# A recurrent hybrid layer on one core: the last product of each seven-product group moved into the next group, with two steps moved from GpSimd to VectorE

## The chip, the cores and the metric

The kernel runs on one core of a Trainium2 chip. A core has TensorE (matmuls into PSUM), VectorE (DVE in the profile), ScalarE (ACT), GpSimd (POOL) and SyncE (SP, which here only issues the DMAs). Each engine works through its own instructions in order and waits at semaphores for the others. The metric is the device time of one execution in microseconds; of the kernel before the median of three runs is 1235.01 us (1233.07 to 1236.85).

## The reference, cut to what matters

One layer of a decoder on 2048 prompt tokens and 8 sequences of 8 sample tokens (2112 in all), width 1024, everything in fp32:

```python
xn = rms_norm(x, norm_pre)
z = xn @ w_in                                    # 1024 -> 4096: v_pool | g_pool | u_lru | g_lru, 1024 each
d = mean over windows 2/4/8/16 of v_pool - v_pool       # one window for each group of 256 channels
y_pool = (d @ pool_w[group]) * pool_scale
xs = causal_conv4(u_lru)                         # depthwise, width 4
r, gi = sigmoid(xs @ wa + ba), sigmoid(xs @ wx + bx)    # block-diagonal, 8 heads of 128
a = exp(-8 * r * softplus(-lam)); u = xs * gi * sqrt(1 - a * a)
h_t = a_t * h_(t-1) + u_t                        # a scan over the tokens
mixed = concat(y_pool * silu(g_pool), h * silu(g_lru))  # 2048 wide
y = x + rms_norm(mixed @ w_out, norm_post)
```

The last rows of the pooling input, of the convolution input and of the scan are returned as well.

## The kernel before, in words

**Split products.** Every fp32 factor of a matmul is kept as a high part (fp32r, a cast) and a low part (the rest, one subtraction), and a product is three matmuls: high x high, high x low, low x high. A "split tile" for weights (`half_tile`, tag `w`) holds the two parts of a 512-deep by 128-wide piece.

**Blocks and quads.** The tokens lie along the free axis and are cut into three blocks of 704 (m = 0, 1, 2), each of two chunks of 352. The columns of `w_in` are cut into quads of 256: four each of V (pool input), G (pool gate), U (lru input) and L (lru gate). A quad of a block is an output of 2 x 128 columns by 2 x 352 tokens with 1024 as the contraction, seen as a 2 x 2 by 2 x 2 product of halves. Block 0 does it plainly, in eight products of 4 x 3 = 12 matmuls (`plain_slot`). Blocks 1 and 2 do it in seven products, the Strassen-Winograd way, from seven combinations of the weights and seven of x, the latter in the slots X11, T1, T2, X22, T3, X21, T4 of the tile XN (high and low part each). Product 1 goes into PSUM bank `a` and is copied to output quarter (0,0); product 6 is added to the same bank, which is copied to (0,1); then 7, which is added to (1,1); then 4, which is copied to (1,0). Products 5 and 3 share bank `e` in the same way, product 2 has bank `d`. So each addition to a bank must wait until the copy or sum of what the bank held is done (`evac` in `quad_slot`: `put_copy` on ACT, line 976; `put_sum` on DVE, line 972). The order of the seven is `ORDER = (1, 5, 6, 3, 7, 2, 4)`. After product 4 `quad_end` starts the quad's chain. Each block has 16 quads. Block 0's first three are done apart; the rest are counted from 0: quads 0 to 12 are of block 0, 13 to 28 of block 1, 29 to 44 of block 2; lasts[0] is quad 12, lasts[1] is quad 28.

**The chains.** Beside the products run generators that name an engine and a planned duration for each step: `pool_chain` (sums of windows on DVE, the high part `dh` on ACT, the low part `dl` on POOL, then four products with `pool_w` whose results are multiplied with the gate, line 1120), `conv_chain` (four taps, line 1145 on ACT and 1156 on DVE, high part `xh` on ACT, low part `xl` on POOL, then the gate products r and i), `lru_chain` (tanh tables; gi + 1 on ACT at line 1197, times xs on POOL at line 1199; exp, sqrt, the scan on DVE at line 1226, the gate on POOL), `silu_chain`, and `x_chain` (the next block's x: loads of tokens into the tiles A and B for the norm, their squares on ACT, then x itself into A and B, the norm's factors, eight scalings on DVE). `transition` then makes the seven split x tiles out of A, B and two "root" tiles.

**What sets the order.** A planner in Python writes all engines' instructions in order. For each slot (one product, `SLOT = 1.94` us planned, or a product and one chain product) `one_slot` emits the product, then the copies of the slot before, then prepares weights, and `run_jobs` grants steps of the chains by the time at which their engine and their input would be free. Counts of free tiles (`t_free`, `e_free`) hold a quad or a chain back: tag `t` has 17 tiles, `e` six, `w` six. A quad begins when two `t` tiles are free (for V: two `e` tiles and the pool chain before). Weights are asked for `AHEAD = 6` products ahead: `w_step` issues the DMA from scratch memory (`wsd`, line 870), or, where a combination is made for the first time, spawns its sums, its split and its store (line 827). All DMAs go through SP's queue in that order, and a DMA whose buffer isn't free holds up those behind it.

After the last quad the output projection (from line 1704 on) multiplies `mixed` with `w_out`, also by seven products, in an order that the framework's scheduler sets. Its accumulators lie in `t` and `e` tiles, its split inputs in `w` tiles.

## Time and profile before

| | |
|---|---|
| median of the runs | 1235.01 us (1233.07 to 1236.85) |
| the profiled execution | 1239.46 us, its span 1237.6 us |
| TensorE busy | 1147.4 us, 93% |
| VectorE busy | 905.7 us, 73% |
| ScalarE busy | 680.5 us, 55% |
| GpSimd busy | 347.1 us, 28% |
| DMA | 322.10 MB, 260 GB/s in the mean |

The stages in the profile: up to about 79 us the first three quads of block 0 with the start of the kernel, up to 312 the rest of block 0, up to about 594 block 1, up to about 880 block 2, then the output projection. A row of the timeline has the start, the duration, engine, line, operation, output<-inputs, shape, count, and in brackets the idle time before it with what ended it. Tile names: a1V is bank `a` of a V quad in block 1, w2L a weight tile of an L quad in block 2, XN an x tile, e, u and g the outputs of V, U and G or L quads. A wait's row has the engine and what it wanted, the releaser, then total us, times and the longest. "issue" is a wait whose releaser the profile doesn't show. SPq is SP's queue of DMAs.

### The profile page before, as it was taken

To read this page: it belongs to the slowest core of one execution; us is meant where nothing else is said; L and a number is where in the kernel's file an instruction comes from. 1 tells how busy PE (TensorE), PEld (TensorE's weight loads), DVE (VectorE), ACT (ScalarE), POOL (GpSimd) and SP (SyncE) were. 2 spreads that over 40 slices of the span, in tenths; PEclk is the share of its full clock that TensorE was granted. 3 is DMA by queue.
4 is the path that set the end of the run, shared out by engine and by line. 5 is a ranking of instruction groups with operands and counts; after the bars stand their busy time and mean duration, and the time that the engine had idled before them with its cause. 6 is when DMAs were issued, how large, how long until landed. Compare 5 with 4: busy or idle time off the path is not lost. (4 is left out here: it accounts for less than half of the span.)

```text
span 1237.6 us, 17847 instructions
## 1 busy us (share of the span) xinstructions
PE 1147.4 (93%) x6274; PEld 1064.7 (86%) x6274; DVE 905.7 (73%) x1308; ACT 680.5 (55%) x1138; POOL 347.1 (28%) x332
## 2 busy tenths in 40 slices
PE   7999996999799899999889889999999999979987
PEld 6999996999799899998789879999878888767866
DVE  6878674784984857688867849686676677768677
ACT  5358664856756747474677556657854233234222
POOL 4223022221351221413542516354120012212232
PEclk9999997999999999998999999999999999989998
DMA  9277894676689788978689999997879676566553
GB/s 336 99 271 271 309 364 163 245 274 229 248 321 375 271 293 282 336 266 307 203 300 339 381 309 359 346 314 276 229 211 264 189 209 192 170 212 189 161 176 120
DMA packets 173305, 322.10 MB, mean 260 GB/s; under 512 B 17504, under 2 KB 79200, under 8 KB 173216
## 3 DMA queue, kind: packets, MB, share of 16 engines
q1 hardware_dynamic: 173216, 320.97, 76.4%
q8 instruction: 49, 0.80, 0.3%
q14 instruction: 40, 0.33, 0.1%
HBM read 218.51 MB, written 102.15 MB: 259 GB/s over the span
## 5 line engine op out<-in xcount | busy, mean ns | idle before, releaser
L437 POOL TENSOR_TENSOR xr<-ac,xr 128x512 f32<-128x512 f32 x27 | 49.5, 1854 | 239.4 <-issue 124.3
L444 PE MATMUL p<-XN,s 128*128 128x512 f32 (+1 forms) x224 | 88.2, 394 | 6.9 <-ACT s L131 6.6
L446 PE MATMUL p<-XN,s 128*128 128x512 f32 (+1 forms) x224 | 88.9, 397 | 5.2 <-DVE s L134 4.5
L1156 DVE SCALAR_TENSOR_TENSOR xs<-u,parT,xs 128x704 f32<-128x704 f32 (+1 forms) x72 | 91.3, 1280 | 1.9 <-ACT xs L1145 1.5
L445 PE MATMUL p<-XN,s 128*128 128x512 f32 (+1 forms) x224 | 87.8, 392 | 1.0 <-DVE XN L309 0.7
L1199 POOL TENSOR_TENSOR ig<-ig,xs 128x704 f32<-128x704 f32 (+1 forms) x24 | 44.8, 1869 | 143.6 <-ACT ig L1197 110.9
L557 ACT ACTIVATE p<-ac 128x512 f32<-128x512 f32 (+1 forms) x32 | 18.8, 588 | 99.2 <-DVE ac L437 98.7
L309 POOL TENSOR_TENSOR dl<-s,dh 128x704 fp32r<-128x704 f32 x24 | 40.6, 1693 | 105.5 <-ACT dh L1092 42.4
L1120 DVE SCALAR_TENSOR_TENSOR g<-y,parT,g 128x352 f32<-128x352 f32 x48 | 27.9, 581 | 56.9 <-PE y L240 56.9
L309 POOL TENSOR_TENSOR xl<-xs,xh 128x704 fp32r<-128x704 f32 (+1 forms) x24 | 48.7, 2030 | 70.1 <-ACT xh L1161 67.4
L240 PE MATMUL zL<-XN,wL 128*128 128x352 f32 x384 | 65.0, 329 | 0.0
L240 PEld LDWEIGHTS zL<-XN,wL 128*128 128x128 f32 x384 | 63.6, 193 | 0.0
L437 DVE TENSOR_TENSOR a<-a,a 128x512 f32<-128x512 f32 x48 | 35.4, 741 | 37.3 <-DMA a<-mixed 29.6
L444 PEld LDWEIGHTS p<-XN,s 128*128 128x128 f32 x224 | 43.3, 193 | 16.9 <-ACT s L131 7.7
L446 PEld LDWEIGHTS p<-XN,s 128*128 128x128 f32 x224 | 43.0, 192 | 16.9 <-DVE s L134 7.3
L131 ACT CAST s<-a 128x512 fp32r<-128x512 f32 x48 | 28.1, 615 | 53.6 <-DVE a L437 52.4
L240 PE MATMUL y<-dh,pw 128*128 128x352 f32 x192 | 54.0, 323 | 0.0
L446 PE MATMUL p<-XN,a 128*128 128x512 f32 x137 | 53.8, 393 | 0.0
L444 PE MATMUL p<-XN,a 128*128 128x512 f32 x137 | 53.6, 391 | 0.0
L445 PE MATMUL p<-XN,a 128*128 128x512 f32 x137 | 53.5, 391 | 0.0
L445 PEld LDWEIGHTS p<-XN,s 128*128 128x128 f32 x224 | 43.1, 192 | 11.3 <-DVE XN L309 1.2
L240 PE MATMUL zG<-XN,wG 128*128 128x352 f32 x288 | 48.8, 330 | 2.7 <-ACT wG L822 2.3
(347 smaller groups left out, 3433.4 us busy)
## 6 DMA issues: line engine op xcount, KB each, us to landing
a<-mixed SPq DMA_DIRECT2D x112, 256.0 KB, 4.2
mixed<-g SPq DMA_DIRECT2D x48, 352.0 KB, 5.6
w2V<-wsd SPq DMA_DIRECT2D x28, 512.0 KB, 4.9
w2G<-wsd SPq DMA_DIRECT2D x28, 512.0 KB, 5.9
w2U<-wsd SPq DMA_DIRECT2D x28, 512.0 KB, 5.8
w2L<-wsd SPq DMA_DIRECT2D x28, 512.0 KB, 6.3
wsd<-XN SPq DMA_DIRECT2D x27, 512.0 KB, 5.7
w1V<-wsd SPq DMA_DIRECT2D x24, 512.0 KB, 5.9
```

The source lines that it names most:

```text
L131: hi_eng.copy(out=hi, in_=src)
L240: nc.tensor.matmul(out, lhsT=lhsT, rhs=rhs, start=start, stop=stop)
L309: (eng or V).tensor_tensor(out=out, in0=a, in1=b, op=ALU.subtract)
L437: (eng or nc.vector).tensor_tensor(out=out, in0=a, in1=b, op=op)
L444: nc.tensor.matmul(out, lhsT=ah, rhs=wh, start=start and k == 0, stop=False)
L445: nc.tensor.matmul(out, lhsT=ah, rhs=wl, start=False, stop=False)
L446: nc.tensor.matmul(out, lhsT=al, rhs=wh, start=False, stop=stop and k == KT - 1)
L557: nc.scalar.activation(out=junk, in_=o, func=AF.Square, accum_out=st[:, g:g + 1])
L1120: V.scalar_tensor_tensor(out=g[:, cs], in0=Y, scalar=col(C_SCALE, blk), in1=g[:, cs], op0=ALU.mult, op1=ALU.mult)
L1156: V.scalar_tensor_tensor(out=xs, in0=E[:, k:k + n], scalar=col(C_CW + 8 * k, b), in1=xs, op0=ALU.mult, op1=ALU.add)
L1199: G.tensor_tensor(out=gi, in0=gi, in1=v, op=ALU.mult)
```

## The change

- **Order of products.** A quad of blocks 1 and 2 now does 1, 5, then product 4 of the quad before, then 6, 3, 2, 7. The first quad of block 1 has no quad before it, the last quad of all does its own 4 at the end. `steps` holds the new order, so weights are loaded by it too. If a quad cannot begin for want of tiles, the pending product 4 is emitted at once (`rest`), before the quad's own first product.
- **VectorE for GpSimd.** `dl`, the pool path's low part, is made by VectorE. The gated input becomes one VectorE instruction, (gi + 1) * xs, in place of one on ScalarE and one on GpSimd.
- **Table-aware order.** `run_jobs` adds 1.3 us to the start of a ScalarE step that needs another activation table, when it compares jobs.
- **x.** The load of a block's x is cut from two DMAs into four of two k-tiles each (eight over the two blocks), with 2.5 us planned after each. The x chain starts at quads 6 and 23 instead of 4 and 14. The turn to block 1 may begin one quad earlier, with X11, T1 and T2 not held back; the turn to block 2 has new slots for its parts, and it stretches over the last quad and the next.
- **Buffers.** `w` has seven tiles instead of six, `t` 16 instead of 17; the output projection's accumulators and one of its short inputs are placed anew to fit.

```diff
--- before.py
+++ after.py
@@ -57,7 +57,8 @@
 HOP = 0.2
 OVER = 0.7
 AHEAD = 6
-ORDER = (1, 5, 6, 3, 7, 2, 4)
+TABLE_COST = 1.3
+X_LEAD = (6, 5)
 XOF = {1: "X11", 6: "T2", 5: "T1", 7: "T3", 4: "T4", 2: "X21", 3: "X22"}
 SLOTS = ("A", "B", "X11", "T1", "T2", "X22", "T3", "X21", "T4")
 KINDS = {"V": 0, "G": 8, "U": 16, "L": 24}
@@ -389,14 +390,14 @@
     def acc_more():
         n = len(acc_all)
         n += 1
-        if n <= T_BUFS - 2:
+        if n <= T_BUFS - 1:
             t = t_tile(f"ac{n}")[:, :PIECE]
-        elif n == T_BUFS - 1:
+        elif n == T_BUFS:
             t = late[:, :PIECE]
-        elif n <= T_BUFS + E_BUFS - 4:
+        elif n <= T_BUFS + E_BUFS - 3:
             t = e_tile(f"ac{n}")[:, :PIECE]
         else:
-            n -= T_BUFS + E_BUFS - 3
+            n -= T_BUFS + E_BUFS - 2
             if n % 2 == 0:
                 acc_pair.append(half_tile(f"acw{n}"))
             t = acc_pair[n // 2][:, n % 2, :].bitcast(F32)
@@ -498,7 +499,7 @@
         n = hi - lo
         ts = []
         for e in range(2):
-            t = t_tile(f"as{q}_{e}", F32R)[:, :PIECE]
+            t = t_tile(f"as{q}_{e}", F32R)[:, :PIECE] if e else x2_box[0][:, 10 * PIECE:11 * PIECE]
             ts.append(t)
             r = stage(f"as{q}_{e}", e).rearrange("p (b t) -> p b t", t=P)[:, :, :n]
             b0 = 8 * q + 4 * e
@@ -782,10 +783,14 @@
             best = None
             for job in jobs:
                 s = fits(job, end)
-                if s is not None and (best is None or s < best[0] - 0.05):
-                    best = (s, job)
+                if s is None:
+                    continue
+                req = job["req"]
+                late = s + (TABLE_COST if len(req) > 2 and table[0] not in TABLES[req[2]] else 0.0)
+                if best is None or late < best[0] - 0.05:
+                    best = (late, s, job)
             if best:
-                grant(best[1], best[0])
+                grant(best[2], best[1])
                 moved = True
 
     def force(job):
@@ -862,9 +867,8 @@
 
     early = []
 
-    def w_step(q, i):
+    def w_step(q, pid):
         m, p, kind = q
-        pid = ORDER[i]
         t = w_tiles[q, pid] = half_tile(f"w{m}{kind}{p}_{pid}")
         if not is_late(q) or pid in (1, 2, 4):
             nc.sync.dma_start(out=flat_of(t).bitcast(F32), in_=w_key(kind, p, pid))
@@ -995,11 +999,8 @@
                 quad_end(q)
         return [("A", 0.45, evac)] if h else []
 
-    def quad_slot(q, i):
-        if q[0] == 0:
-            return plain_slot(q, i)
+    def quad_slot(q, pid):
         t = Q[q]
-        pid = ORDER[i]
         need_w(q, pid)
         w = w_tiles.pop((q, pid))
         key = {1: "a", 6: "a", 7: "a", 4: "a", 5: "e", 3: "e", 2: "d"}[pid]
@@ -1091,9 +1092,9 @@
             dh = e_tile(f"dh{m}_{p}{j}", F32R)[:, :MW]
             AC.copy(out=dh, in_=d)
             yield "?", lambda: e_free() >= 1
-            yield "G", 1.95
+            yield "V", 0.9
             dl = e_tile(f"dl{m}_{p}{j}", F32R)[:, :MW]
-            tsub(dl, d, dh.bitcast(F32), G)
+            tsub(dl, d, dh.bitcast(F32))
             e_live[0] -= 1
             Q[q]["d"].append((dh, dl))
         sums.add((m, p))
@@ -1193,10 +1194,8 @@
         n = MW if m < LM else N_LRU
         lq = (m, p, "L")
         b = 2 * p + j
-        yield "A", 0.89
-        AC.activation(out=gi, in_=gi, func=AF.Identity, bias=ones[:, 0:1])
-        yield "G", 1.95
-        G.tensor_tensor(out=gi, in0=gi, in1=v, op=ALU.mult)
+        yield "V", 0.95
+        V.scalar_tensor_tensor(out=gi, in0=gi, scalar=1.0, in1=v, op0=ALU.add, op1=ALU.mult)
         yield "A", 1.96, "exp"
         AC.activation(out=v, in_=r, func=AF.Exp, scale=nlam[:, b:b + 1], bias=nlam[:, b:b + 1])
         AC.activation(out=r, in_=r, func=AF.Tanh, scale=lam2[:, b:b + 1], bias=lam2[:, b:b + 1])
@@ -1262,9 +1261,12 @@
             for i in part:
                 yield "A", 1.06
                 tok_square(i)
-        yield "D", 0
         for h in range(2):
-            nc.sync.dma_start(out=stage_x(h), in_=xt[:, HK * h:HK * (h + 1), m * MW:(m + 1) * MW])
+            for k in range(0, HK, 2):
+                yield "D", 0
+                nc.sync.dma_start(out=stage_x(h)[:, k:k + 2, :],
+                                  in_=xt[:, HK * h + k:HK * h + k + 2, m * MW:(m + 1) * MW])
+                yield "t", 2.5
         yield "V", 0.2
         yield "A", 0.3, "sqrt"
         tok_rsqrt(tiles[0], tiles[-1] + 1)
@@ -1297,11 +1299,13 @@
         for o, a_, b_ in zip(parts(out), parts(a), parts(b)):
             tsub(o, a_, b_)
 
+    x_macro = [0]
+
     def transition(m):
 
         X = x_quarter
-        at = {0: {"X11": 0, "T1": 0, "T2": 0, "X22": 4, "T3": 5, "X21": 7, "T4": 9},
-              1: {"X11": 1, "T1": 2, "T2": 3, "X22": 4, "T3": 5, "X21": 6, "T4": 7}}[m]
+        at = {0: {"X11": -99, "T1": -99, "T2": -99, "X22": 4, "T3": 5, "X21": 7, "T4": 9},
+              1: {"X11": 1, "T1": 2, "T2": 4, "X22": 5, "X21": 6, "T3": 7, "T4": 10}}[m]
         src = {"X11": X(0, 0), "T1": X(0, 0), "T2": t2_tiles, "X22": X(1, 1), "T3": X(0, 1), "X21": X(1, 0),
                "T4": t2_tiles}
         done = set()
@@ -1333,11 +1337,12 @@
             x_raw(t2_tiles, X(1, 0), t2_tiles)
             x_jobs["X21"] = spawn(put("X21", "G"), T[0], rank=0)
             x_jobs["T4"] = spawn(put("T4"), clock["V"] + HOP, rank=0)
+        x_macro[0] = m + 1
         x_jobs["X11"] = spawn(put("X11"), rank=0)
         x_jobs["sums"] = spawn(chain(), rank=0)
 
     def need_x(n, m):
-        if "sums" not in x_jobs or slot_of[0] < 99:
+        if "sums" not in x_jobs or m != x_macro[0]:
             return
         if n != "X11":
             while n not in x_jobs:
@@ -1611,7 +1616,17 @@
             spawn(conv_chain((0, 0, "U"), j), 4.0)
 
         lasts = [i for i, q in enumerate(QUADS) if i + 1 == len(QUADS) or QUADS[i + 1][0] != q[0]]
-        steps = [(q, i) for q in QUADS if q[0] for i in range(7)]
+        slots, steps = [], []
+        for qi, q in enumerate(QUADS):
+            if q[0] == 0:
+                slots += [(qi, i, q, 0) for i in range(8)]
+                continue
+            seq = [(q, 1), (q, 5)] + ([(QUADS[qi - 1], 4)] if qi - 1 > lasts[0] else [])
+            seq += [(q, pid) for pid in (6, 3, 2, 7)]
+            if qi + 1 == len(QUADS):
+                seq.append((q, 4))
+            slots += [(qi, i, *s_) for i, s_ in enumerate(seq)]
+            steps += seq
         i0 = 8 * (lasts[0] + 1)
 
         def prep(n, qi, i):
@@ -1629,34 +1644,65 @@
             if n < len(steps):
                 w_step(*steps[n])
 
-        for n, (qi, i) in enumerate([(qi, i) for qi, q in enumerate(QUADS) for i in range(7 if q[0] else 8)]):
+        begun = [0, 0]
+
+        def x_turn(n, qi):
+
+            m = begun[0]
+            if m == 2:
+                return
+            if not begun[1]:
+                if m + 1 not in x_ready:
+                    if qi < lasts[m]:
+                        return
+                    while m + 1 not in x_ready:
+                        one_slot(None)
+                if qi < lasts[m] - (m == 0):
+                    return
+                transition(m)
+                begun[1] = 1
+            slot_of[0] = n - first_of[lasts[m]]
+            if slot_of[0] > 12:
+                begun[:] = [m + 1, 0]
+
+        first_of = {}
+        for n, (qi, i, _, _) in enumerate(slots):
+            first_of.setdefault(qi, n)
+        done = set()
+        for n, (qi, i, qp, pid) in enumerate(slots):
             q = QUADS[qi]
             m = q[0]
             if i == 0:
                 while t_free() < {"V": 0}.get(q[2], 2) or (q[2] == "V" and (e_free() < 2 or not sums_done(*q[:2]))):
-                    one_slot(None)
+                    rest = [s_ for s_ in slots[n:n + 3] if m and s_[2] != q and s_[2:] not in done]
+                    if rest:
+                        done.add(rest[0][2:])
+                        run_evacs(evacs)
+                        evacs.clear()
+                        one_slot(lambda: quad_slot(*rest[0][2:]))
+                    else:
+                        one_slot(None)
                 quad_begin(q)
                 while early:
                     force(early.pop())
                 if qi + 1 < len(QUADS) and QUADS[qi + 1][0] == 0:
                     w_raw(QUADS[qi + 1])
-            if i == (5 if m else 0) and qi + 2 < len(QUADS) and is_late(QUADS[qi + 2]):
+            if (pid == 7 if m else i == 0) and qi + 2 < len(QUADS) and is_late(QUADS[qi + 2]):
                 w_raw(QUADS[qi + 2])
-            if (m == 0 and (qi, i) == (4, 0)) or (m == 1 and (qi, i) == (lasts[0] + 2, 4)):
+            if m < LM and (qi, i) == (lasts[m] - X_LEAD[m], 0):
                 spawn(x_chain(m + 1), rank=0)
             if m == 2 and (qi, i) == (lasts[1] + 2, 0):
                 spawn(region_chain(0, "b11", 0, 5), then=[lambda: spawn(combos_chain())])
                 nc.sync.dma_start(out=stc, in_=st_conv)
                 nc.sync.dma_start(out=stl, in_=st_lru)
-            if qi in lasts[:2]:
-                slot_of[0] = i
-                if i == 0:
-                    while m + 1 not in x_ready:
-                        one_slot(None)
-                    transition(m)
-            else:
-                slot_of[0] = 99
-            one_slot(lambda: quad_slot(q, i), lambda: prep(n, qi, i))
+            x_turn(n, qi)
+            if (qp, pid) in done:
+                prep(n, qi, i)
+                continue
+            if pid == 4 and qp == q:
+                run_evacs(evacs)
+                evacs.clear()
+            one_slot(lambda: quad_slot(qp, pid) if m else plain_slot(q, i), lambda: prep(n, qi, i))
 
         def p1_slots(g):
             b = bank["a", g] = new_bank(f"p1_{g}")
@@ -1768,11 +1814,11 @@
             short_out()
 
 
-T_BUFS = 17
+T_BUFS = 16
 RAW_BUFS = 4
 TP_BUFS = 4
 E_BUFS = 6
-W_BUFS = 6
+W_BUFS = 7
 
 _OUTS = [
     ((T_ALL, D), "float32"),
```

## The prediction

> **What bounds the kernel now.** I read the page's busy times first, then the windows by stage, then TensorE's waits, then the timeline around the longest of them.
>
> ```profile
> span 1237.6 us, 17847 instructions
> PE 1147.4 (93%) x6274; PEld 1064.7 (86%) x6274; DVE 905.7 (73%) x1308; ACT 680.5 (55%) x1138; POOL 347.1 (28%) x332
> 79.00:312.00 233.00, 219.71 (x1338) 217.47 (x1337) 165.63 (x222) 152.54 (x253) 57.89 (x51) 0.96 0.72 262
> 312.00:594.00 282.00, 262.53 (x1550) 256.78 (x1549) 212.92 (x262) 171.75 (x265) 85.06 (x73) 0.96 0.86 302
> 594.00:880.00 286.00, 263.50 (x1567) 257.26 (x1566) 207.97 (x261) 183.69 (x276) 116.34 (x128) 0.98 0.89 313
> 880.00:1238.00 358.00, 332.62 (x1432) 267.60 (x1431) 262.38 (x452) 135.90 (x276) 66.14 (x40) 0.97 0.65 190
> ```
>
> TensorE is the bound. The change adds and removes no matmul, so all that can move is TensorE's idle time and the slow spells behind it. Columns of a window are its length, then busy us of PE, PEld, DVE, ACT, POOL, then granted clock, DMA share and GB/s. Block 0 (79 to 312) has 13.3 us of idle TensorE, blocks 1 and 2 (312 to 880), where the product order changes, 568 - 526.0 = 42.0 us, the out-projection (from 880) 25.4 us. Of TensorE's waits from 312 to 880 the short ones on x tiles and weights (total, times, longest), and from its timeline the longest waits of all kinds, each in brackets with its releaser:
>
> ```profile
> PE a2L L238 <- DMA w2L<-wsd: 1.0, 1, 1.0
> PE e2V L238 <- DVE XN L309: 0.9, 1, 0.9
> PE d2V L238 <- DMA w2V<-wsd: 0.9, 1, 0.9
> PE e2L L238 <- DMA w2L<-wsd: 0.8, 1, 0.8
> ```
>
> ```profile
> 317.79 3.38 PE L238 MATMUL e1V<-XN,w1V 128*128 128x352 f32 x11 [3.28 <-DVE XN L309]
> 328.40 2.03 PE L238 MATMUL d1V<-XN,w1V 128*128 128x352 f32 x11 [1.11 <-POOL XN L309]
> 339.38 3.89 PE L238 MATMUL a1G<-XN,w1G 128*128 128x352 f32 x12 [2.96 <-ACT g L976]
> 420.10 2.08 PE L238 MATMUL a1U<-XN,w1U 128*128 128x352 f32 x12
> 422.01 2.08 PE L238 MATMUL e1U<-XN,w1U 128*128 128x352 f32 x12
> 428.01 3.89 PE L238 MATMUL a1U<-XN,w1U 128*128 128x352 f32 x12 [3.91 <-ACT u L976]
> 564.58 3.89 PE L238 MATMUL a1U<-XN,w1U 128*128 128x352 f32 x12 [2.88 <-ACT u L976]
> 610.64 3.05 PE L238 MATMUL a2V<-XN,w2V 128*128 128x352 f32 x12 [3.71 <-issue]
> 700.05 3.66 PE L238 MATMUL a2L<-XN,w2L 128*128 128x352 f32 x12 [2.08 <-DVE g L972]
> 742.02 3.86 PE L238 MATMUL a2V<-XN,w2V 128*128 128x352 f32 x12 [4.82 <-DMA w2V<-wsd]
> 762.97 2.20 PE L238 MATMUL a2G<-XN,w2G 128*128 128x352 f32 x12 [2.40 <-DVE g L972]
> ```
>
> Two things are to be seen. One product is 12 matmuls of 2.08 us, and the next starts 1.92 us later (420.10, 422.01). And after a gap of some 2 to 5 us the next product mostly takes 3.05 to 3.89 us instead of 2.08: the clock is down (after 2.40 us once it was not).
>
> Of the 42.0 us, the split x tiles (XN) take 3.3 + 1.1 + 0.9 = 5.3, weights still in flight 4.8 + 1.0 + 0.9 + 0.8 = 7.5, the unnamed one 3.7. The remaining 25.5 us are accumulations that wait until ACT or DVE (lines 976, 972) has copied the bank out: products 1, 6, 7, 4 share one PSUM bank, 5 and 3 another, and each must be read out before the next adds to it.
>
> **The change part by part.**
>
> **The order.** Before, 1 5 6 3 7 2 4: one product (1.92 us) stands between two on the same bank. After, 1 5 4' 6 3 2 7, with 4' of the quad before: two stand between everywhere. So each of these waits shrinks by 1.92 us. Five are longer, 3.91 + 2.96 + 2.88 + 2.40 + 2.08 = 14.23, of which 14.23 - 5 x 1.92 = 4.6 stays; the others go. Gain 25.5 - 4.6 = 20.9. Their slow spells go too: 3 x (3.89 - 2.08) + (3.66 - 2.08) + (2.20 - 2.08) = 7.1. Together 28.0, 0.9 for each of the 32 quads of blocks 1 and 2.
>
> In sentences of its own: the Trainium skill, "TensorE: Matmul & The Clock Gate", section "Part 1: The HAM clock gate", has the clock fall after an idle window of about 3.4 us, and warns of gaps above 3. By that rule only the 3.91 gap among these five would have paid, and the 7.1 would be 1.8. The gaps of 2.08, 2.88 and 2.96 with 3.66 to 3.89 behind them say otherwise, so the rows decide.
>
> The wait at 610.64 is product 4 too (behind 7's sum on DVE). It had product 2 ahead of it and now has the next quad's 1 and 5, and DVE was late for that sum after one instruction of 3.93 us. I count it whole: 3.71 + (3.05 - 2.08) = 4.7.
>
> ```profile
> 601.51 3.93 DVE L1156 SCALAR_TENSOR_TENSOR xs<-u,parT,xs 128x704 f32<-128x704 f32 x1
> ```
>
> **The price of the order** is that a quad's end, and with it the chains behind it and the release of its two tiles, comes three products (5.8 us) later, while the t tiles go from 17 to 16. Tiles are short already:
>
> ```profile
> L949 POOL COPY u<-hu 128x3 f32<-128x3 f32 x16 | 10.9, 694 | 35.4 <-DVE rg L1226 33.8 <-DVE w L1209 1.6
> 427.51 0.45 ACT L976 COPY u<-a1U 128x352 f32<-128x352 f32 x1 [2.75 <-DVE rg L1226]
> 699.48 0.51 DVE L972 TENSOR_TENSOR g<-a2L,g 128x352 f32<-128x352 f32 x1
> ```
>
> The first write into a U quad's tiles (16 copies, the 8 U quads of blocks 1 and 2) waits for a scan to free them. In the changed code a quad that finds fewer than two free tiles pulls 4' ahead of its own 1, directly behind 7. Then 4' waits at least for the sum (0.51, and 0.57 from its start to the matmul at 700.05), and the quad has the old single cover. I take this for the 8 U quads: 8 x (0.9 not gained + 0.6) = 12.0 lost. Ends: none pulled (0), all 32 at 0.9 + 1.92 (90).
>
> **x pieces and the earlier turn.** Block 1's splits may start a quad earlier, so the waits at 317.79 and 328.40 go: 3.28 + 1.11 + (3.38 - 1.92 for 11 matmuls) = 5.9. Block 2's turn keeps its start; its 0.9 stays. The x chain itself starts later (quad 6 for 4, 23 for 14), so its squares, eight scalings and loads leave the stretches behind quads 4 and 14 and meet others. Each block's x comes in four loads of 0.72 MB instead of two of 1.44 (eight pieces over both blocks), spread over the queue:
>
> ```profile
> 167.72 0.93 SPq L1267 DMA_DIRECT2D XA<-in_xt  x2
> 176.15 7.26 SPq L338 DMA_DIRECT2D wr0U<-in_w_in  x4
> 185.67 0.33 SPq L903 DMA_DIRECT2D pwr<-in_pool_w  x1
> 192.50 0.62 ACT L911 CAST pw<-pwr 128x512 fp32r<-128x512 f32 x1 [12.86 <-DMA pwr<-in_pool_w]
> 193.86 0.66 PE L240 MATMUL r<-xh,lw 128*128 128x352 f32 x1 [8.20 <-ACT xh L1161]
> ```
>
> Here 2.88 MB of x sit ahead of four weight loads, whose issue takes 7.26 us, and of the small pool weights; ACT waits 12.86 us for these with xh queued behind them, and TensorE 8.20. At 302 GB/s the burst is 9.5 us, a piece 2.4. Ends 0 (same bytes through the same engines) and 8.2; I take the middle, 4.1.
>
> **Seven split tiles.** Loads are asked for six products ahead into six buffers, so each waits for the product that has just been issued:
>
> ```profile
> SPq L870 <- PE a2U L238: 23.2, 14, 2.8
> 730.69 6.83 SPq L940 DMA_DIRECT2D sp<-in_st_pool  x2
> 737.61 0.38 SPq L870 DMA_DIRECT2D w2V<-wsd  x1
> ```
>
> With the seventh a load leaves one product (1.92 us) sooner, and what stands behind it on SP with it. The waits of 1.0, 0.9 and 0.8 go; the 4.82 at 742.02, where the state load held the queue for 6.83 us, falls by 1.92. Gain 4.6, upper end 7.5. In the out-projection a seventh tile may help its splits or reshuffle them: 0, ends -5 and +5 out of 25.4 idle.
>
> **Low parts and gated input on DVE.**
>
> ```profile
> L309 POOL TENSOR_TENSOR dl<-s,dh x24: 1421/1613/2143, 80.6 to 840.4; 128x704 fp32r<-128x704 f32 x24
> L1199 POOL TENSOR_TENSOR ig<-ig,xs x24: 1699/1748/2364, 101.4 to 890.8; 128x704 f32<-128x704 f32 x16, 128x728 f32<-128x728 f32 x8
> L1197 ACT ACTIVATE ig<-ig,ones 128x704 f32<-128x704 f32 (+1 forms) x24 | 21.4, 893 | 0.3
> L1074 DVE SCALAR_TENSOR_TENSOR s<-s,e 128x704 f32<-128x704 f32 (+1 forms) x24 | 21.8, 910 | 0.3
> L1156 DVE SCALAR_TENSOR_TENSOR xs<-u,parT,xs x72: 937/962/3929, 78.2 to 860.3; 128x704 f32<-128x704 f32 x48, 128x728 f32<-128x728 f32 x24
> L1156 DVE SCALAR_TENSOR_TENSOR xs<-u,parT,xs 128x704 f32<-128x704 f32 (+1 forms) x72 | 91.3, 1280 | 1.9 <-ACT xs L1145 1.5
> L1212 ACT ACT_TABLE_LOAD x24 | 30.8, 1283 | 0.4
> ```
>
> DVE gains 48 instructions of 0.91 = 43.7 us; ACT loses 21.4; POOL loses 48 of about 1.7 (some 81 of its 259 us from 79 to 880, a third). L1156 costs 91.3 where 72 medians make 69.3: 22 us lost in the slow cases (up to 3.93). If a third of that goes with POOL's third, DVE's net is 36, 6% on the 587 it does from 79 to 880. It is not the bound at 73%; what reaches TensorE lies between 0 and 36, and I take 5, because a bank's sum stands in DVE's queue behind the new instructions.
>
> **Table-aware order** may save some table loads of 1.28 us (24 at one line) and may put a copy behind a chain that needs no load. ACT's lag is counted in the bank waits; I take 0, ends -5 and +5.
>
> **Sum:** 28.0 + 4.7 + 5.9 + 4.1 + 4.6 - 12.0 - 5 = 30.3. The profiled execution took 1239.46 (its span and 1.9 around it) and would take 1209.2. It lies 4.45 above the median 1235.01, so on the runs' scale I forecast 1204.7.
>
> **The rivals.**
>
> **All cover holds** (17%). Nothing is pulled back, the x burst and the weight waits go whole, DVE costs nothing: 28.0 + 4.7 + 5.9 + 8.2 + 7.5 = 54.3, 1181. For it: lru chains lose a POOL and an ACT step, so tiles come free sooner. Against it: the waits for the scan.
>
> **The lag is not cover's** (14%). At 428.01 the copy itself waits 2.75 us for a tile that a scan frees; if such causes stand behind most bank waits, the lag grows with the cover, the 28.0 is not had, and 4.7 + 5.9 + 4.1 + 4.6 - 5 = 14.3 is left: 1221. Against it: most of these waits are under 1.92 us.
>
> **Product 4 pulled back nearly everywhere: slower** (13%). One tile less and two tiles held 5.8 us longer; at the head of most quads fewer than two are free, 4' stands directly behind 7 and waits 1.92 more than with product 2 between. A pulled quad then costs 0.9 + 1.92 = 2.8 against a gain of 42.3 without any (30.3 + 12.0): it decides from 16 of 32 quads. At 23: 64.4 - 42.3 = 22.1 slower, 1257. For it: the 33.8 us of waits for the scan. Against it: in block 1 the two root tiles are held for a far shorter time, since the x chain starts nine quads later.
>
> **The new DVE work reaches TensorE whole** (4%): 36 in place of 5, 1235.0 - (35.3 - 36) = 1235.7. It would if the POOL work that stays (low parts of xs, the gate products) held each new DVE instruction as it held L1156 in its slow cases. Against it: L1156's median of 962 beside its least of 937, so most of its 72 are not held.
>
> Beside it, in sentences of its own: the Trainium skill, "SBUF — State Buffer", section "Who interferes with whom", has a DVE instruction with two SBUF inputs and a GpSimd one that reads SBUF block each other for the whole of the one that came first. All 48 new instructions are of that kind, so this speaks against the change; if each were held for some 1.7 us, DVE would gain 82 us more. L1156's slow cases agree with the rule, its median says how seldom it strikes.
>
> **How the numbers follow.** The forecast has 52%, its own range 1190 to 1220 (half its gain and one and a half of it). 0.3% (3.7 us) is about what a measurement of this kernel can tell from no change. Faster takes the forecast, all cover, and most of the lag case: 80%. Same: the 4% and slivers of its neighbours, 6%. Slower: the pulled case and a little, 14%. The range for 8 in 10 leaves out the far half of the slower case and the best part of the fast one: 1172 to 1240.
>
> **What would show it.** Right: idle TensorE from 312 to 880 near 20 us (42 now); waits of a1, a2 products on ACT and DVE copies below 1 us each; no wait on weights but one; the 3.28 at block 1's first quad gone; DVE some 30 us busier, POOL 80 us less. Wrong: product 4 directly behind 7 in many quads, with a wait at each; new waits of gate or pool products on DVE's low parts; TensorE waiting at block 2's turn for x tiles because its chain started too late; or DVE's slow instructions as many as before.

## The result and the profile after

The changed kernel takes 1193.76 us (median; 1192.5 to 1198.13) where the kernel before took 1234.55 us beside it: a ratio of 0.9674, 95% interval 0.9645 to 0.9703. It is faster by 40.8 us; the forecast was 1204.7 us. Its profiled execution took 1194.03 us. The page's first lines, as for the kernel before:

```profile
span 1192.3 us, 17811 instructions
PE 1132.6 (95%) x6274; PEld 1055.3 (89%) x6274; DVE 902.9 (76%) x1356; ACT 653.8 (55%) x1109; POOL 253.3 (21%) x284
```

For a comparison by stage both traces are cut at the same products: the first one with zV, with a1V, with a2V and with p as its output (block 0 behind its first three quads, block 1, block 2, the out-projection up to TensorE's last matmul). The windows of the kernel before, and then those of the changed kernel, columns as in the prediction:

```profile
79.93:312.27 232.34, 219.23 (x1335) 217.28 (x1335) 164.97 (x221) 151.63 (x250) 58.16 (x51) 0.96 0.72 261
312.27:592.68 280.41, 260.94 (x1541) 255.19 (x1540) 211.33 (x260) 171.60 (x263) 84.37 (x73) 0.96 0.86 302
592.68:874.33 281.65, 259.15 (x1550) 254.02 (x1549) 206.54 (x260) 178.88 (x267) 116.50 (x128) 0.98 0.89 312
874.33:1228.92 354.59, 338.29 (x1457) 272.16 (x1456) 260.17 (x442) 138.89 (x277) 66.39 (x40) 0.98 0.67 194
```

```profile
79.62:311.18 231.56, 220.23 (x1335) 217.77 (x1336) 185.32 (x250) 153.09 (x252) 35.56 (x42) 0.97 0.73 266
311.18:570.19 259.01, 251.65 (x1540) 248.63 (x1539) 196.58 (x266) 170.35 (x266) 45.49 (x54) 0.99 0.91 323
570.19:843.65 273.46, 255.94 (x1555) 252.87 (x1554) 204.23 (x271) 154.92 (x242) 90.81 (x109) 0.98 0.88 324
843.65:1182.47 338.82, 334.64 (x1450) 269.35 (x1450) 253.60 (x443) 135.90 (x271) 59.85 (x38) 0.99 0.69 203
```

Block 0 gives 0.8 us, block 1 21.4, block 2 8.2, and the out-projection 15.8, for which the prediction had taken nothing. These are differences of one execution each, and the one before lies 4.9 us above its median of 1234.55, so they add up to some 46 us where the medians differ by 40.8. In blocks 1 and 2 TensorE's idle time falls from 42.0 to 24.9 us. Its busy time falls too, from 520.1 to 507.6 us for nearly the same matmuls (3091 and 3095 in the windows): 12.5 us less of slow clock. The middle of block 1 has no gap left (windows of 50 us; TensorE is busy for all of each):

```profile
361.00:411.00 50.00, 50.00 (x314) 50.00 (x313) 42.24 (x58) 32.87 (x51) 10.94 (x12) 1.00 0.90 309
411.00:461.00 50.00, 50.00 (x313) 50.00 (x312) 33.76 (x42) 26.27 (x42) 10.40 (x14) 1.00 0.88 297
461.00:511.00 50.00, 50.00 (x314) 50.00 (x313) 32.06 (x41) 33.67 (x51) 8.63 (x12) 1.00 1.02 387
```

TensorE's longest waits in the changed kernel (what it wanted, releaser, total, times, longest; one row of 2.4 us on y is left out):

```profile
PE a2V L239 <- DMA w2V<-wsd: 6.7, 2, 5.8
PE z L241 <- ACT w L1443: 5.4, 1, 5.4
PE e2V L239 <- POOL XN L310: 5.0, 1, 5.0
PE r L241 <- ACT xh L1162: 4.4, 1, 4.4
PE p L445 <- ACT s L132: 3.9, 1, 3.9
PE a1U L239 <- DVE u L976: 2.2, 1, 2.2
```

The waits of a-, e- and d-products on copies and sums (copies are at line 980 here, sums at 976), 25.3 us in the trace before, come to 4.2 us when all rows of this view are added. Of the waits that stood out before, "issue" and the x tiles at block 1's start are gone. But at the turn to block 2 those on x tiles have grown from 0.9 to 6.2 us, and in blocks 1 and 2 those on weights from 7.5 to 8.9. The rest of what is left lies at the kernel's start (z), in block 0 (r) and in the out-projection (p).

### The profile page after: what moved, and what is told of

It is laid out like the page before. It is cut to its first block, busy times and chain, and to the rows that moved or that the text cites. A ratio compares the mean times of both kernels' runs of the same rounds, so it can differ in the third digit from the quotient of the medians.

```text
span 1192.3 us, 17811 instructions
## 1 busy us (share of the span) xinstructions
PE 1132.6 (95%) x6274; PEld 1055.3 (89%) x6274; DVE 902.9 (76%) x1356; ACT 653.8 (55%) x1109; POOL 253.3 (21%) x284
## 5 line engine op out<-in xcount | busy, mean ns | idle before, releaser
L438 POOL TENSOR_TENSOR xr<-ac,xr 128x512 f32<-128x512 f32 x27 | 46.6, 1745 | 225.8 <-DVE ac L578 120.1
L1157 DVE SCALAR_TENSOR_TENSOR xs<-u,parT,xs 128x704 f32<-128x704 f32 (+1 forms) x72 | 85.3, 1193 | 12.0 <-ACT xs L1146 11.6
L310 POOL TENSOR_TENSOR xl<-xs,xh 128x704 fp32r<-128x704 f32 (+1 forms) x24 | 45.9, 1910 | 144.1 <-ACT xh L1162 93.9
L438 DVE TENSOR_TENSOR a<-a,a 128x512 f32<-128x512 f32 x48 | 32.9, 690 | 28.5 <-DMA a<-mixed 24.7
L241 PE MATMUL zU<-XN,wU 128*128 128x352 f32 x288 | 50.3, 329 | 0.0
L241 PE MATMUL zV<-XN,wV 128*128 128x352 f32 x288 | 48.1, 323 | 0.3 <-ACT wV L827 0.2
L241 PEld LDWEIGHTS zU<-XN,wU 128*128 128x128 f32 x288 | 48.1, 194 | 0.0
```

The costliest lines, as they stand in the source:

```text
L241: nc.tensor.matmul(out, lhsT=lhsT, rhs=rhs, start=start, stop=stop)
L310: (eng or V).tensor_tensor(out=out, in0=a, in1=b, op=ALU.subtract)
L438: (eng or nc.vector).tensor_tensor(out=out, in0=a, in1=b, op=op)
L1157: V.scalar_tensor_tensor(out=xs, in0=E[:, k:k + n], scalar=col(C_CW + 8 * k, b), in1=xs, op0=ALU.mult, op1=ALU.add)
```

## The experiments

All times are medians; a ratio is to the kernel before on the same chip in the same stretch of runs, with its 95% interval. Differences between kernels go by the ratios, 1% being 12.3 us. The table has the stages of each profiled execution, cut as above; "w" is the number of split tiles.

| kernel | w | block 0 | block 1 | block 2 | out-projection | time | ratio |
|---|---|---|---|---|---|---|---|
| before | 6 | 232.3 | 280.4 | 281.7 | 354.6 | 1230.7 to 1234.6 | 1 |
| changed | 7 | 231.6 | 259.0 | 273.5 | 338.8 | 1193.8 | 0.9674 |
| old_order | 7 | 231.9 | 254.3 | 284.6 | 337.3 | 1195.4 | 0.9715 [0.9677, 0.9754] |
| six_split | 6 | 231.0 | 258.3 | 276.3 | 349.0 | 1206.4 | 0.9807 [0.9773, 0.9840] |
| on_pool | 7 | 232.7 | 260.1 | 287.0 | 332.1 | 1206.7 | 0.9807 [0.9773, 0.9841] |
| buffers_only | 7 | 239.8 | 295.6 | 271.2 | 332.4 | 1230.6 | 0.9981 [0.9958, 1.0003] |
| gi_only | 6 | 219.6 | 289.2 | 279.0 | 351.3 | 1226.6 | 0.9955 [0.9934, 0.9976] |
| bgi | 7 | 220.5 | 286.0 | 271.5 | 333.5 | 1202.8 | 0.9771 [0.9738, 0.9804] |
| bgitab | 7 | 237.3 | 279.8 | 282.6 | 337.1 | 1225.6 | 0.9944 [0.9924, 0.9964] |
| x_old | 7 | 223.1 | 293.6 | 282.8 | 334.1 | 1226.3 | 0.9949 [0.9931, 0.9968] |
| turn_late | 7 | 231.4 | 302.0 | 280.5 | 335.9 | 1239.6 | 1.0071 [1.0045, 1.0098] |
| lead_14 | 7 | 230.3 | 253.2 | 278.2 | 336.5 | 1191.8 | 0.9694 [0.9660, 0.9729] |
| hop_25 | 7 | 236.0 | 260.3 | 285.5 | 336.3 | 1211.6 | 0.9863 [0.9820, 0.9907] |
| sp_two | 7 | 232.1 | 255.5 | 262.4 | 337.3 | 1180.7 | 0.9596 [0.9554, 0.9638] |

### The order alone undone: old_order

```diff
-            seq = [(q, 1), (q, 5)] + ([(QUADS[qi - 1], 4)] if qi - 1 > lasts[0] else [])
-            seq += [(q, pid) for pid in (6, 3, 2, 7)]
...
+            seq = [(q, pid) for pid in (1, 5, 6, 3, 7, 2, 4)]
...
-            if pid == 4 and qp == q:
-                run_evacs(evacs)
-                evacs.clear()
```

> The changed kernel with the order of the seven products put back to 1 5 6 3 7 2 4; all else stays changed. Theory (the second product of cover is what took the bank waits away): of the 21.4 and 8.2 us that blocks 1 and 2 lost, most come back, TensorE's waits on the copies out of banks a and e rise from about 4 to 20 us or more, and the time is 1215 to 1225. Rival (ACT's lag fell because of the other parts: two steps off ACT and POOL, fewer table loads): bank waits stay below 10 us and the time is below 1203.

It lost 0.4% (5 us), and the intervals of the two ratios overlap; block 1 is 4.7 us shorter, block 2 11.1 longer. In its profile TensorE's waits on copies and sums are as short as with the new order, 4.8 us in all; the longest are these, while the turn to block 2 has grown:

```profile
PE a1V L239 <- ACT e L980: 2.4, 1, 2.4
PE e2G L239 <- ACT g L980: 1.6, 1, 1.6
PE e2V L239 <- POOL XN L310: 7.2, 1, 7.2
```

So with one product of cover, as before, the copies are in time: with the other parts in place the waits are gone without the new order. (Waits on weights are 15.7 us for 8.9.) What the new order would do by itself in the kernel before, no run shows.

### The seventh split tile undone: six_split

```diff
-W_BUFS = 7
+W_BUFS = 6
```

> The changed kernel with six split weight tiles instead of seven. Theory A (the out-projection's gain of 15 us comes from the seventh tile, which lets its next split start sooner): some 15 us back there and 4 to 8 in the blocks, 1210 to 1217. Theory B (the prediction: the tile is worth 4.6 us, in the blocks alone; the out-projection gained by a reshuffle): 1196 to 1201, with the out-projection as short as in the changed kernel.

It lost 1.3% (16 us), between what the two theories gave. By stage, in one execution each, the blocks together are 1.7 us longer (765.7 for 764.0), the out-projection 10.1. There TensorE waits for the splits of its inputs again, and its clock is a little lower, 0.98 for 0.99 (rows of its waits, then the window of the out-projection):

```profile
PE s L453 <- DVE as L135: 3.4, 1, 3.4
PE p L445 <- ACT s L132: 2.1, 1, 2.1
PE p L447 <- DVE s L135: 2.1, 1, 2.1
```

```profile
844.56:1193.51 348.95, 339.72 (x1450) 271.33 (x1450) 257.26 (x443) 136.36 (x271) 62.69 (x38) 0.98 0.67 197
```

The table's column for the out-projection says the same of all fourteen kernels: with six split tiles 349.0 to 354.6 us, with seven 332.1 to 338.8. No kernel lies between. No new order of jobs is behind it either: in this kernel's trace all 6274 matmuls stand in the changed kernel's order, and up to the out-projection the other engines' instructions too, one load in SP's queue aside.

### VectorE's new work given back: on_pool

```diff
-            yield "V", 0.9
+            yield "G", 1.95
...
-            tsub(dl, d, dh.bitcast(F32))
+            tsub(dl, d, dh.bitcast(F32), G)
...
-        yield "V", 0.95
-        V.scalar_tensor_tensor(out=gi, in0=gi, scalar=1.0, in1=v, op0=ALU.add, op1=ALU.mult)
+        yield "A", 0.89
+        AC.activation(out=gi, in_=gi, func=AF.Identity, bias=ones[:, 0:1])
+        yield "G", 1.95
+        G.tensor_tensor(out=gi, in0=gi, in1=v, op=ALU.mult)
```

(In this kernel y comes out other than the reference's; no run shows why. No instruction is left out, so its time is used, with this reserve.)

> The changed kernel with dl again on POOL and the gated input again as an ACT and a POOL instruction. Theory A (the prediction: the move costs up to 5 us, as DVE's queue gets longer): 1189 to 1194. Theory B (the move gains, because DVE is held less by POOL and the chains get shorter): 1199 to 1210, with L1156's kind of instruction back near 1280 ns in the mean and more bank waits.

It lost 1.3% (16 us); by the table block 2 is 13.6 us longer and the out-projection 6.8 shorter. So VectorE's new work did not cost anything that shows; the sign of my 5 us is wrong, or hidden below what a new order of jobs does (hop_25). VectorE's busy time shows something that the prediction had too small. Its 48 new instructions take 45.6 us in the changed kernel, but without them it is as busy, 901.7 us for 902.9 (the page of this kernel):

```profile
PE 1132.8 (94%) x6274; PEld 1054.8 (88%) x6274; DVE 901.7 (75%) x1308; ACT 675.0 (56%) x1132; POOL 330.1 (27%) x332
```

With 77 us more work on GpSimd, the 1308 instructions that VectorE has in both kernels take 44 us longer.

### The buffers alone: buffers_only

The kernel before with the changed kernel's buffers, the accumulators placed to fit, and nothing else:

```diff
-T_BUFS = 17
+T_BUFS = 16
...
-W_BUFS = 6
+W_BUFS = 7
```

> The kernel before with the buffers alone changed: 7 split tiles, 16 t tiles, accumulators placed to fit. Theory A (the seventh tile makes the out-projection shorter): out-projection 340 us instead of 355, time 1213 to 1222. Theory B (worth 4.6 us in the blocks at most, and one t tile less costs some of it): 1228 to 1236.

It gained 0.2%, with 1 inside its interval. But that zero has two halves: the out-projection is 22.2 us shorter, and the blocks, 806.6 us for 794.4, 12.2 longer (the rest of the span moved by 2.0). The losses are in block 1:

```profile
PE r L240 <- ACT xh L1161: 16.3, 3, 8.4
PE a1L L238 <- ACT g L976: 8.6, 2, 8.0
```

### Built up from the kernel before: gi_only, bgi, bgitab

The kernel before with the gated input alone on VectorE; the same with the buffers; the same with the table-aware order as well. The edits are those of the change's diff.

> The kernel before with the gated input alone done on VectorE; seventeen t tiles and six split tiles as before, no other part of the change. Theory T (tiles: the seventh split tile pays in the out-projection and is paid for in the blocks by the t tile given up; the work taken off ScalarE and GpSimd brings the t tiles back sooner and repays that): 1215 to 1226 us, blocks 0 to 2 together 6 to 15 us shorter, the out-projection still 350 to 357 us. Rival X (blocks 1 and 2 gain from the x chain and the turn to the next block, the move itself is worth little): 1228 to 1234 us.

> The kernel before with the gated input on VectorE and with sixteen t tiles, seven split tiles: the two parts that theory T says need each other. T: 1200 to 1212 us, so a gain larger than the 1.4 us of the tiles alone and that of the move alone taken together, the out-projection 330 to 340 us with no waits in it, blocks 0 to 2 together no longer than before. Rival X: 1220 to 1231 us, with the blocks 10 us or more longer than before.

> The run before plus the table-aware order of jobs. T with my zero for the table order: within 4 us of the run without it, and 67 to 72 table loads. Rival B (the table order is worth what its loads cost on ScalarE's path): 5 to 12 us below the run without it, with five or more loads fewer (1.28 us each) and fewer pairs of loads that switch forth and back inside 10 us.

gi_only gained 0.5% (6 us), bgi 2.3% (28 us): more than the two parts alone together (0.5 + 0.2%), as the theory of tiles expected; a new order of jobs may do as much (hop_25). The out-projection gives its 21.1 us as expected, and the blocks are no longer paid for: 778.0 us where the buffers alone had 806.6. But TensorE's waits in bgi are not the short ones which that theory has; one product waits 10.3 us for a step of ScalarE, and those on copies and sums still come to 16.1 us:

```profile
PE a1G L238 <- ACT g L976: 12.8, 3, 6.7
PE y L240 <- ACT xs L1199: 10.3, 1, 10.3
```

bgitab then lost 1.7% (21 us), where both theories had zero or a gain. It has three table loads fewer (65 for 68), 1283 ns each. Three loads are 3.8 us of an engine that is busy for about half the time; 16.8 us were lost in block 0 and 11.1 in block 2, and 6.2 gained in block 1. The rule saves loads and pays nothing here. What it also does is to write all jobs in another order.

### The x parts undone together: x_old

```diff
-X_LEAD = (6, 5)
+X_LEAD = (9, 14)
...
-        at = {0: {"X11": -99, "T1": -99, "T2": -99, "X22": 4, "T3": 5, "X21": 7, "T4": 9},
+        at = {0: {"X11": 0, "T1": 0, "T2": 0, "X22": 4, "T3": 5, "X21": 7, "T4": 9},
-              1: {"X11": 1, "T1": 2, "T2": 4, "X22": 5, "X21": 6, "T3": 7, "T4": 10}}[m]
+              1: {"X11": 1, "T1": 2, "T2": 3, "X22": 4, "T3": 5, "X21": 6, "T4": 7}}[m]
...
-                if qi < lasts[m] - (m == 0):
+                if qi < lasts[m]:
```

and the two large DMAs of x as before. (The x chain of block 1 starts nine quads ahead of the block's end; before the change it was eight.)

> The changed kernel with all its x parts as before: two large x DMAs for a block, the x chain started 9 and 14 quads ahead of a block's end (8 and 14 before), the turn to the next block begun in the block's last quad, and the earlier due slots. Theory T: 1194 to 1203 us (the turn and the pieces are worth under 9 us in all, block 1 under 265 us). Rival X: 1208 to 1222 us, block 1 at 272 us or more. My prediction gave these parts 10.0 us (5.9 and 4.1), so 1204.

It lost 2.8% (34 us), more than either theory had, and all in the blocks: block 1 34.6 us longer, block 2 9.4 longer, block 0 8.5 shorter. The new order of products is in this kernel, and still its waits of a-, e- and d-products on copies and sums come to 18.3 us.

### The turn alone, the start of the x chain alone: turn_late, lead_14

turn_late puts back the slots and the later start of the turn (all below the first "..." of x_old's diff), and keeps the pieces and the later start of the x chain. lead_14 has `X_LEAD = (6, 14)`.

> The changed kernel with the turn to the next block alone as before: begun in a block's last quad (not the last but one) and with the earlier due slots for its sums; the eight x pieces, the later start of the x chain, the table-aware order and all else stay as changed. If the turn is what made block 1 longer by 34.6 us when all x parts were undone: block 1 at 275 us or more and 1205 to 1225 us in all. If it was the start of the x chain or the pieces: block 1 under 264 us, 1191 to 1199 us. My prediction had the turn at 5.9 us: 1200.

> The changed kernel with the x chain for block 2 begun 14 quads ahead of the end of block 1, as about before, not 5; block 0 is the same program. Theory T (t tiles are scarce: that chain holds two of the sixteen from its end to the turn): block 1 10 to 25 us longer, 1203 to 1218 us. If the start does not matter: block 1 within 5 us of 259.0, 1190 to 1199 us. Block 0 within 1 us of 232 either way.

lead_14 is not slower (0.2%, intervals overlap), and its block 1 is 5.8 us shorter, not longer. The theory that t tiles held by the x chain make the blocks long falls.

turn_late lost 4.0% (49 us): block 1 is 43.0 us longer and block 2 7.1, block 0 is not shorter. The turn's own tiles are at most a small part of it. By 311 us the split x tiles had taken 6.4 us of VectorE in the changed kernel and 3.3 in this one, so only some 3 us of that moved into block 1, and at the turn TensorE waits 2.5 + 1.0 us. The rest is farther on, in products of the chains written in TensorE's order ahead of halves that come later than planned. First two rows of the waits of the whole execution (13.2 and 5.0 us of them in block 1), then one place of the timeline on TensorE, and the same on ScalarE:

```profile
PE r L241 <- ACT xh L1162: 17.5, 4, 6.0
PE r L241 <- POOL xl L310: 6.1, 4, 2.7
```

```profile
412.24 0.66 PE L241 MATMUL r<-xh,lw 128*128 128x352 f32 x1 [4.09 <-ACT xh L1162]
415.56 0.66 PE L241 MATMUL r<-xl,lw 128*128 128x352 f32 x1 [2.66 <-POOL xl L310]
```

```profile
408.19 0.45 ACT L980 COPY g<-a1L 128x352 f32<-128x352 f32 x1 [4.83 <-PE a1L L239]
409.44 1.28 ACT L1035 ACT_TABLE_LOAD   x1
411.43 0.76 ACT L1162 CAST xh<-xs 128x704 fp32r<-128x704 f32 x1
```

ScalarE stands idle for 4.83 us waiting for TensorE, and then TensorE for 4.09 us waiting for ScalarE: neither is short of time there, and it is the written order that makes both wait. In the changed kernel no such wait falls between 361 and 511 us.

### A control: hop_25

```diff
-HOP = 0.2
+HOP = 0.25
```

> The changed kernel with one of the planner's assumed times, that of the step from one engine to the next, at 0.25 us for 0.2; no instruction is added, removed or resized, only the written order of the jobs comes out otherwise. If single differences of about 10 us are the parts' own worth: within 3 us of the changed kernel, 1191 to 1197 us. If any edit deals the jobs out anew and that alone moves the time: 5 to 20 us away from it on either side, the slower more likely, with the out-projection within 3 us of 338.8 and the difference in the blocks.

It lost 1.9% (23 us) with no part of the change undone: 4.4 us in block 0, 1.3 in block 1, 12.0 in block 2, the out-projection -2.5. Block 0 has a new hole of 11.9 us:

```profile
PE y L241 <- ACT pw L915: 11.9, 1, 11.9
```

Its timeline shows ScalarE at work throughout; the small cast that TensorE waits for (0.6 us) is written behind some 11 us of other chains' steps. As to noise: lead_14 and sp_two have the changed kernel's program in block 0, and the three took 230.3, 231.6 and 232.1 us. Block 1 of sp_two is the changed kernel's too, and took 255.5 us for 259.0. So an execution repeats a block to some 4 us, while an edit that shifts the planner's clock deals the jobs out anew and moved the time by 23 here (lead_14, another such edit, by 0.2%). The 16 us of on_pool, the 21 of bgitab and the 5 of old_order are inside that. six_split and sp_two are not of this kind: by their traces the instructions of every engine stand in the changed kernel's order, in six_split up to the out-projection and with one load aside.

### Two buffers for the state loads: sp_two

```diff
-tag="sp", bufs=1
+tag="sp", bufs=2
...
-        s8 = sb.tile([P, 6, NH], F32, name="s8")
+        s8 = late[:, 0:6 * NH].rearrange("p (a b) -> p a b", b=NH)
```

> The changed kernel with two buffers in place of one for the state loads of block 2 (the statistics tile of the start is laid over another tile to make room), so that the state load does not hold the sync engine's queue, 10.8 us at the turn to block 2, with block 2's weights behind it. If the hold is the cause of the waits of 5.0 and 5.8 us on TensorE in block 2: those go, with the slower clock behind them, block 2 at 258 to 267 us and 1181 to 1189 us in all. If the late halves come from GpSimd and VectorE anyway: block 2 within 4 us of 273.5, 1190 to 1197 us.

The ratio is 0.9596 [0.9554, 0.9638], below the changed kernel's interval: 1180.7 us, the fastest of all. Block 2 is 11.0 us shorter, as the first theory had it, and no product of a V quad waits more than 1.0 us for weights there (one of a G quad waits 1.8). In the changed kernel the issue of the state loads on SP's queue at the turn to block 2, and TensorE at the second such place:

```profile
568.83 10.84 SPq L944 DMA_DIRECT2D sp<-in_st_pool  x2
```

```profile
706.89 3.57 PE L239 MATMUL a2V<-XN,w2V 128*128 128x352 f32 x11 [5.82 <-DMA w2V<-wsd]
```

In this kernel the same issue, and the window of block 2:

```profile
565.19 1.80 SPq L944 DMA_DIRECT2D sp<-in_st_pool  x2
```

```profile
566.54:828.96 262.42, 253.60 (x1556) 251.72 (x1555) 202.86 (x271) 155.07 (x242) 90.74 (x109) 0.99 0.92 338
```

10.84 us of a held queue, with block 2's weights behind it, became 1.80. The wait for the low part of an x tile on GpSimd is 3.2 us where the changed kernel has 5.0; these 3.2 are not the queue's. In the changed kernel the second load had to wait for GpSimd to copy out the first, and that copy took 5.82 us (last section).

## Why the prediction was right, and where it was wrong

**The total** was right in sign and near in size, 30.3 of 40.8 us, and by stage blocks 1 and 2 came out near too: the terms for them make 26.2, the trace shows 29.6. The out-projection was missed (15.8 for 0), block 0 was put too high (0.8 for 4.1). That the sum came so near is luck in part: its largest term rests on a mechanism that the runs don't bear out, and several others were wrong in opposite directions.

**The order, 28.0: the waits went, but they go without the new order too.** The forecast was that 4.6 us of bank waits stay; 4.2 did, and the slow clock behind them went. The step that failed is "each of these waits shrinks by 1.92", which takes the copy's time as fixed and the cover as the only thing that changes. Without the new order 4.8 us stay (old_order), and with the new order but the old turn or x parts 13.6 (turn_late) and 18.3 (x_old). How late a copy is depends on what stands ahead of it on ScalarE and VectorE. The rival "the lag is not cover's" came nearer to this cause, with a tile that a scan frees as its example; but its price was wrong, since the 28.0 was had all the same.

**The price of the order, 12.0:** I had counted a product 4 pulled ahead of its follower's first product in 8 of 32 quads. It happened once, in block 1's last U quad, and there TensorE waited 2.22 us for the sum, where I had 0.6. So this term was some 2 to 3 us:

```profile
555.52 2.19 PE L239 MATMUL a1U<-XN,w1U 128*128 128x352 f32 x12 [2.22 <-DVE u L976]
557.55 0.64 PE L239 MATMUL a1L<-XN,w1L 128*128 128x352 f32 x3
```

**"Issue", 4.7:** the wait is gone, as forecast.

**The turn, 5.9, and the x pieces, 4.1:** the x waits at block 1's first quad are gone, which is what the 5.9 counted; at block 2's turn, where 0.9 was to stay, there are 6.2. But undoing the turn costs 49 us, of which 3.5 are waits at the turn; a sum over waits that exist could not see the rest. Of the pieces, block 0 shows nothing: the 8.20 us behind the pool weights became 4.42 at another place, and with the old x parts block 0 is 8.5 us shorter. How much of that is the pieces' and how much the turn's place was not measured by itself.

**The seventh tile, 4.6 in the blocks and 0 in the out-projection:** the step looked for a late weight load and took the tile's second use, the out-projection's split inputs, as neutral. It is the other way round: undoing the tile alone costs 1.7 and 10.1, and all the buffers together shorten the out-projection by 22.2. The waits on weights in blocks 1 and 2, of which 4.6 were to go, did not fall (7.5 before, 8.9 now). The rows were there, TensorE's waits for as and s in the stage whose 25.4 us of idle time I had counted (the kernel before):

```profile
PE p L444 <- ACT s L131: 6.6, 2, 5.5
PE p L446 <- DVE s L134: 5.5, 6, 2.7
PE s L452 <- DVE as L134: 2.3, 1, 2.3
```

**VectorE's new work, -5:** its two new groups took 45.6 us, 2 more than costed, and none of it shows as a loss. The step that failed is the net of 36 us on VectorE: its busy time did not rise by some 30 us, it fell from 905.7 to 902.9. GpSimd's 80 us went as forecast (347.1 to 253.3 in all). Line 1156's mean fell from 1280 to 1193 ns, 6.0 us in all against the 7 that I had taken. But that line was not the only one to gain: VectorE's other 1308 instructions became 48.4 us shorter together, the eight that combine x tiles alone 8.4 (15.2 to 6.8). Whether the move gains by itself, as on_pool and gi_only hint, is left open: both differences are smaller than hop_25's.

**The table order, 0:** the load count fell from 70 to 65. No run shows a gain from it.

What stays open is which part the 30 us of the blocks belong to. The parts don't add up: undone one by one they cost 5, 16, 16, 34 and 49 us (the turn is in the last two), far above the 41 of all together. Nearly every such edit gives another written order, the one of the changed kernel is a good one, and hop_25 shows that it is lost by an edit that means nothing.

## What to carry to other kernels

Where a planner writes the order of all engines, change one of its constants by a little and time that first: the spread it gives (here 23 us, from one constant) is the least that a part undone must exceed before its difference is called the part's own. An edit that leaves every engine's order as it was (six_split, sp_two) needs no such margin. A buffer's worth lies where its rows of waits are, in every stage that uses its tag, and a zero in the total can be a gain in one stage and a loss in another, so cut both traces at the same products before judging. A queue of DMAs held by a load with one buffer shows as a long issue row with other loads behind it, and a second buffer there was worth some 10 us.

## What the runs showed of the hardware that was not expected

**GpSimd's copy behind VectorE.** A copy of 128x120 on GpSimd took 5.82 us in the changed kernel's turn to block 2, and the next of the same shape 0.29, the median of the eight (its timeline, then the first and the last of VectorE's rows beside it):

```profile
573.49 5.82 POOL L945 COPY e<-sp 128x120 f32<-128x120 f32 x1 [35.22 <-DMA sp<-in_st_pool]
581.16 0.29 POOL L945 COPY e<-sp 128x120 f32<-128x120 f32 x1 [1.72 <-DMA sp<-in_st_pool]
```

```profile
573.47 1.69 DVE L310 TENSOR_TENSOR XA<-XA 128x704 f32<-128x704 f32 x2
578.28 0.88 DVE L310 TENSOR_TENSOR rt<-XA,rt 128x704 f32<-128x704 f32 x1
```

From 573.47 to 579.16 VectorE ran seven instructions with two inputs in SBUF, back to back, and the copy ended 0.15 us behind the last. The Trainium skill, "SBUF — State Buffer", section "Who interferes with whom", has a VectorE instruction with two inputs in SBUF contend with a GpSimd instruction that reads SBUF, over a shared pair of ports that is an exclusive lock. The rows agree, and they show more: a run of such instructions without a gap kept GpSimd out for its whole length. (Spans on GpSimd are rough; one case was looked at.)

**A slow clock behind short gaps, once and not again.** In the changed kernel, after gaps of 1.54 and 0.93 us with a few short matmuls between and behind them, two products took 3.72 and 2.68 us for 2.08:

```profile
324.79 0.43 PE L241 MATMUL r<-xh,lw 128*128 128x352 f32 x1 [1.54 <-ACT lw L915]
326.31 0.95 PE L241 MATMUL r<-xh,lw 128*128 128x352 f32 x2 [0.93 <-DVE lw L310]
327.65 3.72 PE L239 MATMUL a1G<-XN,w1G 128*128 128x352 f32 x12
331.17 2.68 PE L239 MATMUL e1G<-XN,w1G 128*128 128x352 f32 x12
```

In sp_two, the same matmuls in the same order, with nearly the same gaps, kept their speed:

```profile
324.74 0.43 PE L241 MATMUL r<-xh,lw 128*128 128x352 f32 x1 [1.61 <-ACT lw L915]
326.18 0.59 PE L241 MATMUL r<-xh,lw 128*128 128x352 f32 x2 [0.86 <-DVE lw L310]
326.93 2.09 PE L239 MATMUL a1G<-XN,w1G 128*128 128x352 f32 x12
328.85 2.08 PE L239 MATMUL e1G<-XN,w1G 128*128 128x352 f32 x12
```

The granted clock from 311 to 361 us was 0.93 in the changed kernel and 1.00 in sp_two. The Trainium skill, "TensorE: Matmul & The Clock Gate", section "A second HAM failure mode: psum-queue depth-cycling", tells of a bf16 kernel in which TensorE idles briefly but often between groups of matmuls, and the clock swings. The changed kernel's rows look like that, sp_two's do not. So the slow clock behind such a cluster cost 2.2 us (1.64 + 0.60) in one execution and nothing in the other; the lengths of the gaps do not decide it, and what does is not shown. Some 2 of the 3.5 us by which sp_two's block 1 is shorter are this.
